# New issue times for blocks, sums, turns and attention steps in a two-layer trunk

## The chip, the cores and the metric

One core of a Trainium2 chip runs the kernel. The time is device microseconds of one execution; a kernel's time is the median of its runs. The engines are TensorE (PE, matmuls), VectorE (DVE), ScalarE (ACT), GpSimd (POOL) and SyncE (SP, which only issues transfers here). All times below are in microseconds.

## The reference

A trunk of two layers over 256 frames with 2048 features, 16 heads of 128, and an MLP width of 8192, all in float32:

```python
u = rms_norm(h, a_norm_g[l])
q, k, v, fz = jnp.split(u @ a_w_in[l], [D, 2 * D, 3 * D], axis=-1)
...                                   # q, k: rms_norm per head
logf = jax.nn.log_sigmoid(fz.astype(jnp.float32) + a_b_f[l].astype(jnp.float32))
o = forgetting_attention(q, k, v, logf)      # causal softmax, logits + cumulated logf
h = h + o.reshape(B, S, D) @ a_w_out[l]
h = h + sq_relu_mlp(h, mlp_norm_g[layer], mlp_w1[layer], mlp_w2[layer])
kv = rms_norm(h, kv_norm_g) @ kv_w           # shared keys and values
...
q = rms_norm((u @ b_w_q[l]).reshape(B, S, H, Dh), b_q_g[l])
o = chunked_relbias_attention(q, k_sh, v_sh, b_rel[l])
h = h + o.reshape(B, S, D) @ b_w_out[l]
h = h + sq_relu_mlp(h, mlp_norm_g[layer], mlp_w1[layer], mlp_w2[layer])
```

with `sq_relu_mlp(h, g, w1, w2) = square(relu(rms_norm(h, g) @ w1)) @ w2`. All weights together are read once; they are most of the traffic.

## The kernel before

**The matmuls.** A float32 product is made of three passes over rounded parts. ACT rounds a piece of weights (128 x 1024) to `hi` (L312), DVE takes the rest `lo = raw - hi` (L313), and PE runs hi times the activation's hi (L579), hi times its lo (L581) and lo times its hi (L583). One such piece with its two splits is a unit; `fetch` and `top_up` keep two or three units split ahead of PE.

**The pairs.** Two neighbouring blocks of output columns form a `Pair`. A part of its rows is multiplied in seven products in place of eight, of sums of blocks. The blocks are 11, 12, 21, 22 (loaded by SP, L911, in `bring`); the sums are T3 = 22 + 12 and T2 = T3 + 11 (DVE, L937, in `make`), T1 = 12 + 11 and T4 = T2 + 21 (in most pairs transfers of POOL that add block to block in place, L946, in `put`). The seven units of forms come in the order 11, T3, T2, T1, 21, T4, 22. T4 overwrites T2, and its transfer can be issued only when T2 has been split. `Pair.units` holds six numbers: how many plain units before the pair's first form unit the loads of 12, 22, 21 and 11, the sum T3 and the sum T1 are issued. A larger number is earlier.

**The stages.** Attention A (its projection with `plan_heads`, its softmax steps in between, its output with `plan_out`), MLP A (`plan_mlp`: pairs of the first matrix and of the second take turns), the query projection, the shared keys and values, attention B, its output, MLP B. Suffixes H and K in the tables name the two halves (H: attention A and MLP A, K: attention B and MLP B). In an MLP the first pair is "early" (W1E), the second pair of the first matrix is W1I, the rest use W1F, W1S, W2F, W2S, W2L.

**The filling steps.** Work beside the matmuls (softmax, normalization, sums of activations for the products, turns of hidden activations) is cut into steps, and `run_fill` takes steps off a queue at certain units (HM and KM: how many at each unit; ATA, ATB, LONG, SHORT, T0H, T0K: which place in the queue each step has). A turn transposes 32 x 32 blocks on DVE (L427) and moves the blocks between partitions, either by a `hop` (sixteen small transfers, L453, eight each on SP and POOL) or by a `carry` (one write to DRAM, L437, and four reads, L443).

**What sets the order.** The instructions on DVE, ACT, PE and SP are kept in the order in which the code writes them (`keep_order`), so each table fixes an order by hand: whatever stands behind a waiting instruction on its engine waits too.

Of the kernel before, what the change touches and what calls it, by code (L numbers as in the profile page):

```python
# [27 lines left out]
UN = 1024  # L28
AHEAD = 2
TABLES = {  # L30
    "ATA": ((11, 13, 15, 19, 10), (9, 12, 16, 18, 10), (8, 13, 15, 19, 9), (9, 9, 12, 12, 10)),
    "ATB": ((10, 13, 14, 18, 9), (9, 13, 15, 16, 11), (10, 12, 15, 17, 10), (7, 10, 12, 12, 9)),
# [13 lines left out]
    "LONG": ((0, 1, 2, 5, 9, 11, 11, 14, 14), (0, 0, 0, 4, 7, 9), (1, 0, 1, 3, 5, 5), (2, 0, 1, 2, 4, 5)),  # L46
    "OFH": (12, 8, 2, 7, 5, 5),
    "OFK": (11, 10, 5, 6, 8, 4),
    "ORD": {"deep1": "a4 F b4 F a5 F a6 a7", "qkv": "a2 a3 a4 F a5 F a6 F a7 b2 b3 b4", "ahead0": "F a4 F a5 a6 a7 F b4",
        "kv": "a2 F a3 a4 a5 F a6 a7 F b2 b3 b4", "deep0": "a4 F F F b4 a5 a6 a7", "ahead1": "a4 F F a5 a6 a7 F b4"},  # L50
    "OSH": (10, 11, 5, 6, 4, 2),
    "OSK": (8, 8, 6, 7, 4, 2),
    "OUTH": "F a2 a3 a4 a5 F b2 b3 F b4 G b5 G a6 a7 G b6 b7 G c2 G c3 G c4 c5 G c6 c7 d2 d3 d4",
    "OUTK": "a2 a3 F b2 a4 b3 F a5 F b4 b5 G G a6 a7 G b6 G c2 b7 G c3 G c4 c5 d2 G c6 c7 d3 d4",
    "QF": (4, 7, 1, 4, 2, 2),
    "QS": (10, 5, 4, 8, 3, 1),
    "SHORT": ((2, 0, 1, 4, 7, 7, 9, 9, 12), (2, 2, 3, 3, 7, 7, 8, 11, 13), (0, 1, 1, 4, 7, 7), (0, 0, 0, 2, 4, 4)),
# [13 lines left out]
    "XOH": (9, 12, 13, 10),  # L71
    "XOK": (9, 14, 12, 14),
    "XS": (2, 5, 4, 1),
}
EARLY = 3
LAZY = ("qkv", "kv", "out0", "out1")
# [3 lines left out]
DEEP = 2 * UN  # L80
WIDE1 = (1, 2, 3, 4, 5, 6, 7)
# [15 lines left out]
def trunk(ctx: ExitStack, tc: tile.TileContext, xT, xr, gs, hg, bf, wgate, w_in, w_oa, w1a, w1fa, w1sa, w2fa, w2sa,  # L97
          w_kv, w_qb, w_ob, w1b, w1fb, w1sb, w2fb, w2sb, rel, out):
    nc = tc.nc
    V, S, G, TE, SY = nc.vector, nc.scalar, nc.gpsimd, nc.tensor, nc.sync  # L100

    def pool(name, bufs, **kw):
        return ctx.enter_context(tc.tile_pool(name=name, bufs=bufs, **kw))
# [5 lines left out]
    qkv = pool("qkv", 2)  # L109
# [82 lines left out]
    def plan_mlp(w1, w1f, w1s, w2f, w2s, rest, when, more=None):  # L192
        pairs = []

        def add(w, wf, ws, i, wides, order, times, cols=WIDE):
            j = wides.index(i) if i in wides else i - sum(1 for k in wides if k < i)
            names = ("11", "12", "21", "22")
            if i in wides:
                m = 8 - cols // 512
                src = [[None] * (8 - m) + [ws[m * (2 * j + q) + u] for u in range(m)] for q in range(2)]  # L200
                big = {k: wf[4 * j + m] for m, k in enumerate(names)}
            else:
                src = [[w[16 * j + 8 * q + u] for u in range(8)] for q in range(2)]
                big = {k: src[int(k[1]) - 1][int(k[0]) - 1] for k in names}
            pairs.append(Pair(big, src, order, len(pairs) % 2 == 1, times, cols if i in wides else UN))

        rooms = {"12": "v0", "22": "k0", "11": "k1", "21": "v1"}
        seq = [(0, 0, 0), (0, 0, 1)]
        for c in range(NCH):
            seq += [(1, c, 0)] + [(0, c + 1, 0)] * (c + 1 < NCH) + [(1, c, 1)] + [(0, c + 1, 1)] * (c + 1 < NCH)  # L210
        for m, (second, c, q) in enumerate(seq):
            i = 2 * c + q
            if second:
                add(None, w2f, w2s, i, WIDE2, "deep%d" % q, TABLES["W2L" if i == 7 else "W2S" if q else "W2F"], DEEP)
            else:
                add(w1, w1f, w1s, i, WIDE1, "ahead%d" % q if i else "early", TABLES["W1E" + when] if not i else TABLES["W1I" + when] if i == 1 else TABLES["W1S" if q else "W1F"], DEEP)
            pairs[-1].at = second, c, q
        if more is not None:
            for q in range(2):
                add(more, None, None, q, (), "" if q else "query", TABLES["QS" if q else "QF"])  # L220
                pairs[-1].at = 1, NCH, q
        plan, rest = join(pairs, rooms, rest)
        return queue(plan + rest)

    def queue(plan):
        units.extend(Form(p, i, q == 3) if q > 1 else p.src[q][i] for p, q, i in plan)
        return plan

    def join(pairs, rooms, rest):
        plan = []  # L230
        for p in pairs:
            p.rooms = rooms
            if p.order != "early":
                rooms = {"12": rooms["11"], "22": rooms["12"], "11": rooms["21"], "21": rooms["22"]}
            mine, rest = p.plan(rest)
            plan += mine
        return plan, rest
# [33 lines left out]

    plan_h, rest, tail_h = plan_heads(w_in, "H", w_oa)
    plan_a = plan_mlp(w1a, w1fa, w1sa, w2fa, w2sa, rest, "H", w_qb)
    plan_k, rest, tail_k = plan_heads(w_kv, "K", w_ob)
    plan_b = plan_mlp(w1b, w1fb, w1sb, w2fb, w2sb, rest, "K")
    ready = deque()

# [118 lines left out]
    def room(tag, name, dtype=F32):  # L396
        return qkv.tile([P, DEEP], dtype, name=name, tag=tag, bufs=1)
# [72 lines left out]
    LONG, SHORT, SHORT2 = TABLES["LONG"], TABLES["SHORT"], TABLES["SHORT2"]  # L470
# [351 lines left out]
    early = room("bias", "early")  # L822
# [521 lines left out]
```

## Time and profile before

| what | value |
|---|---|
| median of 3 runs | 2069.12 us (2067.84 to 2071.15) |
| profiled execution | 2071.87 us, span 2070.1 us |
| granted clock of PE, mean | 0.999 |
| busy PE, DVE, ACT, POOL | 99%, 86%, 68%, 12% of the span |
| traffic | 556.20 MB, mean 269 GB/s |

A busy share is an average over stages with different limits; the waits of PE, which is busy for nearly the whole span, are read in the stage where they lie. Transfers are listed by the engine that issued them, with the time from issue to landing.

### The profile page before, as it was taken

To read this page: it belongs to the slowest core of one execution; us is meant where nothing else is said; L and a number is where in the kernel's file an instruction comes from. 1 tells how busy PE (TensorE), PEld (TensorE's weight loads), DVE (VectorE), ACT (ScalarE), POOL (GpSimd) and SP (SyncE) were. 2 spreads that over 40 slices of the span, in tenths; PEclk is the share of its full clock that TensorE was granted. 3 is DMA by queue.
4 is the path that set the end of the run, shared out by engine and by line. 5 is a ranking of instruction groups with operands and counts; after the bars stand their busy time and mean duration, and the time that the engine had idled before them with its cause. 6 is when DMAs were issued, how large, how long until landed. Compare 5 with 4: busy or idle time off the path is not lost.

```text
span 2070.1 us, 27097 instructions
## 1 busy us (share of the span) xinstructions
PE 2050.1 (99%) x9068; PEld 1689.7 (82%) x9068; DVE 1776.8 (86%) x2058; ACT 1398.8 (68%) x1799; POOL 243.9 (12%) x355
## 2 busy tenths in 40 slices
PE   9999999999999999999999999999999999999999
PEld 7888878878888888888888888888788888888887
DVE  6788788889899899899888678888998988988996
ACT  6766566667677677676778566667766675776764
POOL 1111010021101102101012011100211111111020
PEclk9999999999999999999999999999999999999999
DMA  9898888788889898897988888888888888888885
GB/s 328 258 278 273 265 262 268 281 263 256 284 270 284 252 299 274 243 286 251 285 253 262 290 260 265 256 264 284 277 284 270 267 267 286 259 284 260 288 261 148
DMA packets 174221, 556.20 MB, mean 269 GB/s; under 512 B 40688, under 2 KB 68992, under 8 KB 151040
## 3 DMA queue, kind: packets, MB, share of 16 engines
q1 hardware_dynamic: 153344, 463.94, 62.8%
q0 software_dynamic: 20448, 89.96, 21.9%
q8 instruction: 71, 1.16, 0.2%
q14 instruction: 70, 0.57, 0.1%
q10 hardware_dynamic: 288, 0.57, 0.1%
HBM read 514.50 MB, written 26.76 MB: 261 GB/s over the span
## 4 chain that ended last, share of the span: by engine, by line
PE 82%; DMA 6%; issue 5%; DVE 4%; ACT 1%; SPq 1%; POOL 0%; DVEq 0%; ACTq 0%; POOLq 0%
PE acc L579 19%; PE acc L583 19%; PE acc L581 19%; PE s L583 7%; PE s L579 7%; PE s L581 7%; DVE lo L313 2%; DMA wT<-in_w1fa 2%; ACT hi L312 1%; DMA raw<-in_w_in 1%; PE po L751 1%; DMA wT<-in_w1fb 1%; PE po L714 1%; DMA w<-in_w2fb 1%; DMA turn<-z 0%
## 5 line engine op out<-in xcount | busy, mean ns | idle before, releaser
L313 DVE TENSOR_TENSOR lo<-raw,hi 128x1024 fp32r<-128x1024 f32 (+1 forms) x414 | 500.0, 1212 | 94.6 <-ACT hi L312 86.2
L312 ACT ACTIVATE hi<-raw 128x1024 fp32r<-128x1024 f32 (+1 forms) x414 | 434.7, 1054 | 198.1 <-PE acc L581 134.2
L579 PE MATMUL acc<-hi,act 128*128 128x512 f32 x1784 | 500.1, 393 | 8.1 <-ACT hi L312 7.6
L583 PE MATMUL acc<-lo,act 128*128 128x512 f32 x1784 | 494.4, 390 | 1.3 <-DVE lo L313 1.0
L581 PE MATMUL acc<-hi,act 128*128 128x512 f32 x1784 | 493.8, 390 | 0.0
L579 PEld LDWEIGHTS acc<-hi,act 128*128 128x128 f32 x1784 | 333.4, 188 | 79.3 <-ACT hi L312 10.1
L583 PEld LDWEIGHTS acc<-lo,act 128*128 128x128 f32 x1784 | 334.1, 188 | 74.8 <-DVE lo L313 5.9
L581 PEld LDWEIGHTS acc<-hi,act 128*128 128x128 f32 x1784 | 335.3, 188 | 70.7 <-DVE act L370 0.5
L312 ACT ACTIVATE hi<-w 128x1024 fp32r<-128x1024 f32 x258 | 271.1, 1058 | 127.9 <-PE acc L581 86.5
L313 DVE TENSOR_TENSOR lo<-wT,hi 128x1024 fp32r<-128x1024 f32 x220 | 267.1, 1221 | 74.7 <-ACT hi L312 71.0
L313 DVE TENSOR_TENSOR lo<-w,hi 128x1024 fp32r<-128x1024 f32 x258 | 310.0, 1217 | 20.1 <-ACT hi L312 18.8
L312 ACT ACTIVATE hi<-wT 128x1024 fp32r<-128x1024 f32 x220 | 232.2, 1059 | 114.1 <-PE acc L581 51.8
L579 PE MATMUL s<-hi,act 128*128 128x512 f32 x530 | 146.4, 391 | 0.0
L583 PE MATMUL s<-lo,act 128*128 128x512 f32 x530 | 145.3, 389 | 0.7 <-DVE lo L313 0.7
L581 PE MATMUL s<-hi,act 128*128 128x512 f32 x530 | 144.8, 388 | 0.0
L453 POOL DMA_DIRECT2D q<-z x200 | 99.4, 512 | 251.8 <-DVE z L427 212.0
L583 PEld LDWEIGHTS s<-lo,act 128*128 128x128 f32 x530 | 99.0, 188 | 22.6 <-DVE lo L313 2.4
L581 PEld LDWEIGHTS s<-hi,act 128*128 128x128 f32 x530 | 99.4, 188 | 20.6
L579 PEld LDWEIGHTS s<-hi,act 128*128 128x128 f32 x530 | 99.1, 188 | 20.8 <-ACT hi L312 0.4
L579 PE MATMUL s<-hi,S 128*128 128x512 f32 x288 | 89.5, 392 | 0.0
L583 PE MATMUL s<-lo,S 128*128 128x512 f32 x288 | 88.9, 390 | 0.1
L581 PE MATMUL s<-hi,S 128*128 128x512 f32 x288 | 88.7, 389 | 0.0
(213 smaller groups left out, 2235.8 us busy)
## 6 DMA issues: line engine op xcount, KB each, us to landing
raw<-in_w_in SPq DMA_DIRECT2D x75, 512.0 KB, 5.8
w<-in_w2fa SPq DMA_DIRECT2D x32, 1024.0 KB, 6.4
w<-in_w2fb SPq DMA_DIRECT2D x32, 1024.0 KB, 6.2
w<-in_w1fa SPq DMA_DIRECT2D x28, 1024.0 KB, 7.2
w<-in_w1fb SPq DMA_DIRECT2D x28, 1024.0 KB, 7.0
raw<-in_w2sa SPq DMA_DIRECT2D x52, 512.0 KB, 7.7
raw<-in_w_kv SPq DMA_DIRECT2D x52, 512.0 KB, 5.2
raw<-in_w2sb SPq DMA_DIRECT2D x51, 512.0 KB, 7.0
```

Of the source, the lines that this page charges most:

```text
L312: S.activation(hi[:, c], raw[:, c], AF.Copy)
L313: V.tensor_tensor(lo[:, c], raw[:, c], hi[:, c].bitcast(F32), op=ALU.subtract)
L453: (G if i % 2 else SY).dma_start(dst[32 * j : 32 * j + 32, i * n : (i + 1) * n], z[32 * i : 32 * i + 32, j * n : (j + 1) * n])
L579: TE.matmul(ps[:, cols], xh, cut(hi, j), start=first, stop=False, **kw)
L581: TE.matmul(ps[:, cols], xl, cut(hi, j), start=False, stop=False, **kw)
L583: TE.matmul(ps[:, cols], xh, cut(lo, j), start=False, stop=last, **kw)
L714: TE.matmul(s[:, P : 3 * P], q[:, a, P:T], k[:, a], start=True, stop=True)
L751: TE.matmul(po[:, :T], v[:, 0, a * P : (a + 1) * P], pT[:, :2], start=True, stop=False)
```

## The change

Numbers in the tables of the two attention stages, the output projections and the entries of the MLPs are set anew; the tables of the MLPs' steady part stay (W1F, W1S, W2F, W2S, T). The second pair of an MLP's first matrix gets an order of its own, "second", with the same contents as the one it used. One turn of MLP B is made by a carry in place of a hop (the second number of T0K's third row, where -1 means a hop). The work is otherwise the same, instruction for instruction. Some of the lines:

```diff
-    "OFH": (12, 8, 2, 7, 5, 5),
+    "OFH": (11, 10, 1, 7, 7, 7),
...
-    "T0K": ((0, -1, 5, 5, 6, 6, 6, 7, 10), (1, -1, 4, 5, 6, 6, 6, 8, 8), (1, -1, 6, 6, 7, 7), (0, -1, 5, 5, 5, 5)),
+    "T0K": ((0, -1, 5, 5, 6, 6, 6, 7, 10), (1, -1, 5, 5, 6, 6, 7, 8, 8), (1, 3, 6, 7, 7, 7), (0, -1, 4, 4, 4, 4)),
...
-    "W1IH": (11, 7, 6, 7, 3, 2),
-    "W1IK": (10, 6, 2, 9, 4, 2),
+    "W1IH": (11, 7, 6, 9, 4, 1),
+    "W1IK": (11, 7, 3, 9, 4, 3),
...
-                add(w1, w1f, w1s, i, WIDE1, "ahead%d" % q if i else "early", TABLES["W1E" + when] if not i else TABLES["W1I" + when] if i == 1 else TABLES["W1S" if q else "W1F"], DEEP)
+                add(w1, w1f, w1s, i, WIDE1, ("second" if i == 1 else "ahead%d" % q) if i else "early", TABLES["W1E" + when] if not i else TABLES["W1I" + when] if i == 1 else TABLES["W1S" if q else "W1F"], DEEP)
```

The changed file is one line longer, so a line there has a number one higher than the same line before.

Three places in the order. The first is SP just ahead of the forms of MLP A's second pair. `w11`, `w22` and `w21` are that pair's blocks, `raw` and `zraw` plain units, `turn` and `q` the last turn of attention A's output. Before:

```order
L437 DMA turn_3643<-z_3639 128x1024
L291 DMA raw_3659<-in_w1a 128x1024
L291 DMA raw_3695<-in_w1a 128x1024
L443 DMA q_3640<-turn_3643 32x4x256 x4
L911 DMA w22_3713<-in_w1fa 128x2048
L911 DMA w11_3715<-in_w1fa 128x2048
L291 DMA raw_3727<-in_w1a 128x1024
```

And after:

```order
L438 DMA turn_3643<-z_3639 128x1024
L912 DMA w11_3645<-in_w1fa 128x2048
L292 DMA raw_3661<-in_w1a 128x1024
L292 DMA raw_3693<-in_w1a 128x1024
L444 DMA q_3640<-turn_3643 32x4x256 x4
L912 DMA w22_3715<-in_w1fa 128x2048
L292 DMA raw_3727<-in_w1a 128x1024
```

The load of block 11 moved ahead of two plain units and the four reads of the turn.

The second place is DVE in attention A, about 105 us into the span. `row` and `pbuf` belong to the softmax of earlier heads, `t` to that of the next ones, `acc` is a sum in an accumulator of the running pair (L976). Before:

```order
L313 TENSOR_TENSOR lo_996<-raw_866,hi_995 128x1024
L734 RECIPROCAL row_968<-row_968 128x2
L736 TENSOR_SCALAR pbuf_123<-pbuf_123,row_968 128x128
L736 TENSOR_SCALAR pbuf_123<-pbuf_123,row_968 128x256
L427 STREAM_TRANSPOSE pbuf_123<-pbuf_123 128x3x4x32
L723 SCALAR_TENSOR_TENSOR t_1017<-po_990,cq_753,nb_803 128x128
L725 TENSOR_REDUCE row_1018<-t_1017 128x1
L723 SCALAR_TENSOR_TENSOR t_1017<-po_990,cq_753,nb_803 128x256
L725 TENSOR_REDUCE row_1018<-t_1017 128x1
L976 SCALAR_TENSOR_TENSOR acc_1034<-acc_921,p7_980 128x512
L313 TENSOR_TENSOR lo_1038<-R_358,hi_1037 128x1024
L313 TENSOR_TENSOR lo_1046<-raw_904,hi_1045 128x1024
```

And after:

```order
L314 TENSOR_TENSOR lo_989<-raw_877,hi_988 128x1024
L977 SCALAR_TENSOR_TENSOR acc_1020<-acc_927,p7_980 128x512
L314 TENSOR_TENSOR lo_1024<-R_358,hi_1023 128x1024
L735 RECIPROCAL row_968<-row_968 128x2
L737 TENSOR_SCALAR pbuf_123<-pbuf_123,row_968 128x128
L737 TENSOR_SCALAR pbuf_123<-pbuf_123,row_968 128x256
L428 STREAM_TRANSPOSE pbuf_123<-pbuf_123 128x3x4x32
L724 SCALAR_TENSOR_TENSOR t_1031<-po_1008,cq_753,nb_794 128x128
L726 TENSOR_REDUCE row_1032<-t_1031 128x1
L724 SCALAR_TENSOR_TENSOR t_1031<-po_1008,cq_753,nb_794 128x256
L726 TENSOR_REDUCE row_1032<-t_1031 128x1
L314 TENSOR_TENSOR lo_1042<-raw_903,hi_1041 128x1024
```

The accumulator's sum and one split moved ahead of the eight softmax instructions.

The third place is DVE some 150 us later, at the first output pair of attention A. `wT3` is that pair's sum T3, `y` a sum of head outputs. Before:

```order
L427 STREAM_TRANSPOSE pbuf_123<-pbuf_123 128x3x4x32
L313 TENSOR_TENSOR lo_2490<-raw_2355,hi_2489 128x1024
L937 TENSOR_TENSOR wT3_2507<-R_238,R_358 128x1024
L313 TENSOR_TENSOR lo_2517<-raw_2402,hi_2516 128x1024
L1083 TENSOR_TENSOR y_2525<-act_1211 128x256 x4
```

And after, where the sum now stands:

```order
L314 TENSOR_TENSOR lo_2399<-raw_2292,hi_2398 128x1024
L938 TENSOR_TENSOR wT3_2417<-R_238,R_358 128x1024
L314 TENSOR_TENSOR lo_2427<-wT3_2112,hi_2426 128x1024
L735 RECIPROCAL row_2341<-row_2341 128x2
L737 TENSOR_SCALAR pbuf_123<-pbuf_123,row_2341 128x128
```

T3 moved ahead of two groups of softmax instructions and four splits.

More of the change, by code (lines that the diff above doesn't have):

```diff
@@ L30 @@
 TABLES = {
-    "ATA": ((11, 13, 15, 19, 10), (9, 12, 16, 18, 10), (8, 13, 15, 19, 9), (9, 9, 12, 12, 10)),
-    "ATB": ((10, 13, 14, 18, 9), (9, 13, 15, 16, 11), (10, 12, 15, 17, 10), (7, 10, 12, 12, 9)),
[1 row of a table removed]
+    "ATA": ((11, 13, 15, 19, 9), (9, 12, 16, 18, 11), (8, 13, 15, 19, 9), (9, 9, 12, 12, 10)),
+    "ATB": ((10, 13, 14, 18, 9), (9, 13, 15, 17, 11), (9, 12, 15, 17, 10), (7, 10, 12, 12, 9)),
[1 row of a table added]
     "GS": (1,),
[11 rows of a table removed]
-    "LONG": ((0, 1, 2, 5, 9, 11, 11, 14, 14), (0, 0, 0, 4, 7, 9), (1, 0, 1, 3, 5, 5), (2, 0, 1, 2, 4, 5)),
-    "OFH": (12, 8, 2, 7, 5, 5),
[L48 to L57, printed above, removed]
[1 row of a table removed]
[11 rows of a table added]
+    "LONG": ((0, 1, 2, 5, 9, 10, 11, 14, 14), (0, 0, 0, 4, 7, 9), (1, 0, 1, 2, 5, 5), (1, 0, 1, 4, 5, 5)),
+    "OFH": (11, 10, 1, 7, 7, 7),
+    "OFK": (10, 9, 4, 9, 8, 4),
[3 rows of a table added]
+    "OSH": (7, 9, 7, 5, 5, 1),
+    "OSK": (9, 7, 4, 7, 5, 1),
+    "OUTH": "F a2 a3 b2 a4 a5 b3 b4 F G F G b5 a6 a7 G b6 b7 G c2 G c3 G d2 c4 c5 G c6 c7 d3 d4",
+    "OUTK": "a2 a3 F b2 a4 F b3 a5 F b4 b5 G G a6 a7 G b6 G c2 b7 d2 G c3 G c4 c5 c6 G c7 d3 d4",
+    "QF": (4, 4, 2, 3, 2, 1),
+    "QS": (10, 4, 4, 8, 3, 1),
+    "SHORT": ((4, 0, 0, 3, 6, 8, 8, 9, 12), (2, 2, 3, 3, 7, 7, 8, 10, 13), (2, 0, 0, 2, 6, 7), (0, 0, 0, 2, 4, 5)),
[1 row of a table added]
     "T": ((1, -1, 5, 14, 14, 14, 15, 20, 20), (0, 2, 8, 10, 10, 14, 18, 20, 22), (0, -1, 5, 6, 7, 7), (0, -1, 4, 5, 5, 5)),
[4 rows of a table removed]
[4 rows of a table added]
     "W1F": (7, 5, 1, 5, 4, 3),
[2 rows of a table removed]
[2 rows of a table added]
     "W1S": (8, 6, 4, 5, 4, 1),
     "W2F": (6, 5, 1, 5, 4, 3),
[1 row of a table removed]
[1 row of a table added]
     "W2S": (7, 7, 4, 5, 3, 1),
-    "XOH": (9, 12, 13, 10),
+    "XOH": (9, 12, 13, 11),
     "XOK": (9, 14, 12, 14),
-    "XS": (2, 5, 4, 1),
+    "XS": (0, 5, 6, 2),
 }
```

35 rows, old and new, of the table TABLES are left out of this document.

## Prediction

> **What bounds the kernel now.** I read the head of the page, then the waits of PE (the engine of the matmuls), then the timeline around each wait.
>
> ```profile
> span 2070.1 us, 27097 instructions
> PE 2050.1 (99%) x9068; PEld 1689.7 (82%) x9068; DVE 1776.8 (86%) x2058; ACT 1398.8 (68%) x1799; POOL 243.9 (12%) x355
> PE acc L579 <- ACT hi L312: 7.6, 6, 3.4
> PE acc L583 <- DVE lo L313: 2.6, 3, 1.2
> PE acc L579 <- DVE acc L976: 1.4, 1, 1.4
> PE acc L579 <- ACT pbuf L731: 1.1, 1, 1.1
> PE pt L138 <- DVE mhalf L140: 1.1, 1, 1.1
> PE s L583 <- DVE lo L313: 0.7, 2, 0.4
> ```
>
> PE is busy for 99% of the span and the change keeps every matmul, so PE's own work is a floor. What a new order can win is the waits. The columns of the last six lines are total us, times, longest: together 14.5 us. The change can only move these, or make new ones. Where they lie (start, duration, instruction, in brackets the idle time before it and its releaser):
>
> ```profile
> 107.05 0.47 PE L579 MATMUL acc<-hi,S 128*128 128x512 f32 x1 [1.13 <-ACT pbuf L731]
> 279.39 0.49 PE L583 MATMUL acc<-lo,act 128*128 128x512 f32 x1 [0.99 <-DVE lo L313]
> 442.21 0.92 PE L579 MATMUL acc<-hi,act 128*128 128x512 f32 x2 [3.37 <-ACT hi L312]
> 1465.34 0.73 PE L579 MATMUL acc<-hi,act 128*128 128x512 f32 x2 [1.18 <-ACT hi L312]
> 1481.81 0.50 PE L583 MATMUL s<-lo,act 128*128 128x512 f32 x1 [0.37 <-DVE lo L313]
> 468.68 0.50 PE L583 MATMUL acc<-lo,Sh 128*128 128x512 f32 x1 [0.40 <-DVE lo L313]
> ```
>
> The longest costs more than its wait. In the windows below (PE busy with count, PEld, DVE, ACT, POOL, granted clock, DMA share, GB/s) the clock falls to 0.83 right behind it.
>
> ```profile
> 400.00:410.00 10.00, 10.00 (x46) 8.28 (x45) 3.62 (x4) 5.16 (x9) 0.00 (x0) 1.00 1.00 407
> 420.00:430.00 10.00, 9.95 (x44) 7.73 (x43) 9.97 (x10) 6.96 (x9) 2.47 (x5) 1.00 0.79 222
> 430.00:440.00 10.00, 8.84 (x40) 6.98 (x38) 8.40 (x12) 5.84 (x6) 3.46 (x7) 1.00 1.01 269
> 440.00:450.00 10.00, 7.79 (x27) 6.23 (x28) 7.16 (x7) 8.09 (x9) 0.50 (x1) 0.83 0.75 276
> 1460.00:1470.00 10.00, 8.75 (x37) 6.35 (x36) 8.63 (x12) 6.95 (x9) 0.97 (x2) 1.00 0.87 267
> ```
>
> 46 matmuls fill 10 us, 0.217 us each. From 442.21 to 450 there are 7.8 us, room for 36, and 27 ran: 9 x 0.217 = 2.0 us lost to the clock. The wait of 442.21 is therefore worth 3.37 + 2.0 = 5.4 us, and the ceiling for the whole change is 14.5 + 2.0 = 16.5 us.
>
> **Part 1, the second pair of MLP A (W1IH, T0H).** The chain of waits and the timeline name a transfer, the POOL accumulate that makes form T4:
>
> ```profile
> 426.83 14.17 DMA wT<-in_w1fa
> 595.83 11.11 DMA wT<-in_w1fa
> 923.01 11.48 DMA wT<-in_w1fa
> wT<-in_w1fa POOLq DMA_DIRECT2D x7, 1024.0 KB, 9.2
> 426.83 0.92 POOL L946 DMA_DIRECT2D wT<-in_w1fa  x1 [2.69 <-DVE lo L313]
> 431.61 10.69 SPq L453 DMA_DIRECT2D q<-z  x8
> 397.51 0.85 SPq L911 DMA_DIRECT2D w<-in_w1fa  x2
> 390.61 0.33 SPq L437 DMA_DIRECT2D turn<-z  x1
> ```
>
> It left at 426.83 and landed at 441.00, after 14.17 us, where its likes took 11.11 and 11.48 when they were late and 9.2 in the median (last column). Around it the DMA engines were full (share 1.01 from 430 to 440) while 420 to 430 still had a fifth free; the sixteen turn pieces issued from 431.61 share them. The change brings the load of the 1 MB block "11", one of the two issued at 397.51, forward past two raw loads and the reads of a turn, right behind the row of 390.61: some 6.5 us sooner. It leaves the full stretch of 400 to 410, where DVE worked 3.62 us of 10, waiting for what comes behind. Also the T3 sums move ahead of a weight split, into that idle time. I take DVE's chain and the turn behind it to run 2 us earlier, which leaves more of the traffic before 430. T4 itself can hardly leave sooner: POOL waited 2.69 us for the split of the form that T4 overwrites, and that split goes at PE's pace. So I take 11.5 us, the row of 923.01, for its flight: it lands at 438.3, and the wait falls from 3.37 to 3.37 - 2.7 = 0.7. The window of 1460 to 1470, with its wait of 1.18, kept the clock at 1.00, so the 2.0 us go too. Gain 2.7 + 2.0 = 4.7; I take 4.4, since what lands sooner here has to be split sooner too. Bounds 0 (it still takes 14.17) and 5.4 (9.2 lands at 436.0, and 3.37 before 441.0 is 437.6).
>
> The Trainium skill, "DMA: Bandwidth & Descriptors", section "Queues, rings and completion order", says that each DMA engine takes turns between the queues it has work for, a packet at a time. By that T4's share depends on whether SP's queue has work at all, not on how much, and a load that left earlier helps only if SP's queue then runs empty; the sum would lose the 4.4. The row of 14.17 against 9.2 speaks for a share that varies, but not for which cause. This is the first rival.
>
> **Part 2, attention A's steps (ATA, ATB, HM).** The profile names ACT's L731 as the releaser at 107.05, but on DVE the sum of L976, which frees the bank that the matmul writes, ended at 106.91, just ahead of it:
>
> ```profile
> 103.54 0.16 DVE L734 RECIPROCAL row<-row 128x2 f32<-128x2 f32 x1
> 106.22 0.69 DVE L976 SCALAR_TENSOR_TENSOR acc<-acc,p 128x512 f32<-128x512 f32 x1
> 107.94 1.22 DVE L313 TENSOR_TENSOR lo<-raw,hi 128x1024 fp32r<-128x1024 f32 x1
> ```
>
> Between 103.54 and 106.22 stand eight softmax instructions, 2.7 us; they hold up L976. The change puts L976 and one split ahead of the eight, so the wait of 1.13 goes. What is late next is the split behind the eight (the row of 107.94, ended at 109.16): it ends about as before, but PE is there 1.1 us sooner; I charge 0.3. Net 0.8; bounds -0.3 (if ACT's L731 was the releaser after all) and 1.1.
>
> **Part 3, first output pair of A (OFH).** The T3 sum leaves a stretch in which DVE has no pause for one in which it had some:
>
> ```profile
> 264.86 1.22 DVE L937 TENSOR_TENSOR wT<-R 128x1024 f32<-128x1024 f32 x1
> 254.55 1.23 DVE L313 TENSOR_TENSOR lo<-wT,hi 128x1024 fp32r<-128x1024 f32 x1 [0.66 <-ACT hi L312]
> 261.33 1.23 DVE L313 TENSOR_TENSOR lo<-R,hi 128x1024 fp32r<-128x1024 f32 x1 [1.40 <-ACT hi L312]
> ```
>
> It moves to just ahead of the row at 254.55. Of its 1.22 us, 0.66 fall into that pause, the rest into the one of 1.40 before 261.33; up to there it delays two splits by up to 1.2 us. DVE then reaches 279 up to 1.22 us sooner, and PE's wait there is 0.99. I take 1.0; bounds 0 and 1.2.
>
> **Part 4, MLP B's second pair (W1IK) and its sums (T0K).** T4 of this pair gated PE at 1465.34. The order of DVE and SP from 1441 to 1465 stays; only T1's accumulate and the load of "21" before it come earlier, so some of the traffic is gone sooner: 0.4 of 1.18, bounds 0 and 1.2. Behind it four sums move from ahead of the split that PE waited for to behind two splits:
>
> ```profile
> 1477.88 0.41 DVE L382 TENSOR_TENSOR sum<-q 128x256 f32<-128x256 f32 x1
> ```
>
> Four of 0.41 are 1.6 us, more than the 0.37 that PE waited at 1481.81: gain 0.4.
>
> **Part 5, the rest.** One hop (sixteen small transfers) of MLP B becomes a write to DRAM and four reads, all on SP:
>
> ```profile
> 1480.68 4.99 SPq L453 DMA_DIRECT2D q<-z  x8
> 1495.81 1.04 ACT L1009 ACTIVATE q<-q 128x1024 f32<-128x1024 f32 x1
> turn<-z SPq DMA_DIRECT2D x35, 512.0 KB, 5.2
> q<-turn SPq DMA_DIRECT2D x68, 128.0 KB, 5.6
> ```
>
> A write at 1480.7 and reads behind it land 5.2 + 5.6 later plus SP's rows between, at 1492 to 1494, before ACT wants them at 1495.81: nothing, and without that cover the difference, up to 2 us on ACT, which is not PE's bound there. At 468.68, in the pair behind Part 1, the split that PE waits for keeps its place, with ACT and DVE steps of the activation now ahead of it: cost 0.2. About thirty weight loads leave 1 to 9 us later in the issue order; those I followed keep their cover, because the split they feed is 2 to 6 us ahead of PE. One that doesn't costs about what the smaller waits above cost, 0.4 to 1.2; I charge one, 0.8 (bounds 0 and 4).
>
> **The sum.** 4.4 + 0.8 + 1.0 + 0.4 + 0.4 - 0.2 - 0.8 = 6.0 us. The profiled execution took 2071.87 us (span 2070.1 and 1.8 around it), 2.75 above the median of 2069.12; it becomes 2065.9, and the median 2063.1.
>
> **The rivals.**
>
> *T4 does not land sooner.* The moved megabyte was long down when T4 left, and SP's queue still has the turn and the blocks of the second matrix to send. For it: 0.79 share in 420 to 430 says the engines had no backlog from 400 then. Against it: the chain ahead of the turn starts sooner. The gain is 6.0 - 4.4 = 1.6, time 2067.5, within 0.2%. Chance 0.18.
>
> *T4 takes longer, and it ends slower.* If the turn's sixteen pieces are done sooner, SP goes on sooner to what now follows:
>
> ```profile
> 442.41 1.00 SPq L911 DMA_DIRECT2D w<-in_w2fa  x2
> ```
>
> These two 1 MB loads left just after T4 had landed. Issued 3 us sooner they run beside T4's last part. With 2 MB at the 407 GB/s of the fullest window its flight grows by 5.2 us, PE waits 8.6 and the low clock lasts twice as long: +5.2 + 2.0, less the other gains' 1.6, is 5.6 us slower, 2074.7. Against it: SP issues them only when their buffers are free. It decides from a landing at 442.6 on (441.0 plus those 1.6). Chance 0.10, with 0.08 more for a late load elsewhere that does the same to PE.
>
> **How the numbers follow.** Forecast (T4 lands sooner and no new wait beyond the one charged): 2063.1, chance 0.64. All upper bounds together are 5.4 + 1.1 + 1.2 + 1.2 + 0.4 = 9.3, plus the run's own spread of 1.3 to 2.0: low end 2057.5. The high end takes in the first rival with its spread and the lighter part of the second: 2072. About a fifth is left outside. 0.2% is 4.1 us, what a measurement of this kernel can tell from no change; the line is at 2065.0 and 2073.3. The forecast's own range, 2058 to 2067, lies partly above 2065.0; I give 0.54 of its 0.64 to faster and 0.10 to same, which with the first rival makes 0.28. The second rival and its kin are the 0.18 of slower.
>
> **What would show it.** In the profile after: the accumulate of "wT" issued near 425 lands in under 12 us; PE's wait behind it is under 1 us; the clock is 1.00 in every window of the second pair. No wait on L731 near 107, none on L313 near 279 and near 1480. I am wrong if the total of PE's waits does not fall below 9 us, if a new wait above 1.5 us stands on ACT's L312 behind a load or an accumulate, or if the clock drops anywhere else.

## The result and the profile after

The changed kernel takes 2063.25 us (median of 7 runs, 2061.24 to 2066.70) against 2070.95 (7 runs, 2064.83 to 2071.26) on the same chip. The ratio is 0.9971, 95% interval 0.9961 to 0.9982: 6.0 us faster, between 3.7 and 8.1 (the two medians lie 7.7 apart; the ratio takes in all the runs). The forecast was 2063.1. The profile after is of the fastest of its seven executions (2061.24), the one before of an execution slower than any of its seven (2071.87), so the two spans lie 10.7 us apart and show more than the gain.

The head of the page and the waits of PE in the profile after (line numbers are one higher):

```profile
span 2059.4 us, 27087 instructions
PE acc L580 <- ACT hi L313: 3.9, 6, 1.4
PE acc L584 <- DVE lo L314: 2.3, 3, 1.0
PE pt L139 <- DVE mhalf L141: 1.1, 1, 1.1
PE s L584 <- DVE lo L314: 0.3, 1, 0.3
PE acc L580 <- ACT act L756: 0.2, 1, 0.2
```

The listed waits fell from 15.3 us (the 14.5 shown before and three small ones) to 7.8, and the longest from 3.4 to 1.4. The waits on L976 and L731 are gone. The one on L976 stood at 1745 us, in the steady part of MLP B, whose tables stay; E1, E6, E8 and E10 below, which leave MLP B as before, don't have it either, so its end is not the change's gain. The place behind the T4 accumulate of MLP A's second pair, in the timeline, the list of transfers (last column: us to landing) and the windows:

```profile
421.24 0.93 POOL L947 DMA_DIRECT2D wT<-in_w1fa  x1 [4.17 <-DVE lo L314]
wT<-in_w1fa POOLq DMA_DIRECT2D x1, 1024.0 KB, 12.4
434.88 0.50 PE L580 MATMUL acc<-hi,act 128*128 128x512 f32 x1 [1.37 <-ACT hi L313]
430.00:440.00 10.00, 8.57 (x37) 6.48 (x36) 9.53 (x12) 7.31 (x9) 0.50 (x2) 1.00 0.86 268
440.00:450.00 10.00, 10.00 (x46) 8.29 (x45) 9.83 (x11) 6.77 (x7) 0.92 (x1) 1.00 0.87 288
```

T4 flew 12.4 us and not 14.17, PE waited 1.37 and not 3.37, and the clock stayed at 1.00: 46 matmuls in the window that held 27. Read from these two profiles alone, Part 1 of the prediction looks right. The experiments say otherwise.

### The profile page after: what moved, and what is told of

It is laid out like the page before. It is cut to its first block, busy times and chain, and to the rows that moved or that the text cites. A ratio compares the mean times of both kernels' runs of the same rounds, so it can differ in the third digit from the quotient of the medians.

```text
span 2059.4 us, 27087 instructions
## 1 busy us (share of the span) xinstructions
PE 2047.2 (99%) x9068; PEld 1689.5 (82%) x9068; DVE 1777.7 (86%) x2058; ACT 1399.3 (68%) x1799; POOL 238.8 (12%) x347
## 3 DMA queue, kind: packets, MB, share of 16 engines
q8 instruction: 71, 1.16, 0.2%
## 4 chain that ended last, share of the span: by engine, by line
PE 91%; DVE 3%; issue 2%; DMA 2%; ACT 1%; SPq 0%; ACTq 0%; POOL 0%; DVEq 0%; POOLq 0%
PE acc L584 21%; PE acc L580 21%; PE acc L582 21%; PE s L580 9%; PE s L582 9%; PE s L584 9%; DVE lo L314 1%; DMA wT<-in_w1fb 1%; PE po L715 1%; PE po L752 1%; ACT hi L313 1%; DMA q<-turn 0%; DMA raw<-in_w2sb 0%; PE po L714 0%; PE po L753 0%
```

## The experiments

Each was run beside the kernel before on one chip; ratios are to that. Before's own median was between 2068.57 and 2070.95 in these comparisons, so the ratio with its interval counts and not the difference of two medians from different ones.

**E1: W1IH alone.**

```diff
-    "W1IH": (11, 7, 6, 7, 3, 2),
+    "W1IH": (11, 7, 6, 9, 4, 1),
```

> The kernel before with only W1IH from the change. Theory (the T4 accumulate of MLP A's second pair lands sooner because the load of block 11, T3's sums and what follows them come earlier): the wait near 440 falls from 3.37 to about 1.5 us and the clock stays at 1.00 behind it, 4 us faster than before (2065 to 2067), all other waits as before. Rival (the other tables of attention A bring it, by an earlier SP and DVE ahead of the pair): the wait stays above 3 us and the clock falls, within 1 us of before.

Ratio 1.0014 (1.0004 to 1.0025): 2.9 us slower. The wait behind T4 fell to 2.18, but another stood ahead of it. Timeline of E1 (PE, ACT) and its list of transfers for the turn's reads; then the same two rows of before:

```profile
409.84 0.50 PE L579 MATMUL acc<-hi,act 128*128 128x512 f32 x1 [1.75 <-ACT hi L312]
406.05 0.51 ACT L404 ACTIVATE y<-q,gsb 128x256 f32<-128x256 f32 x1 [3.99 <-DMA q<-turn]
q<-turn SPq DMA_DIRECT2D x4, 128.0 KB, 9.7
```

```profile
400.61 1.71 ACT L404 ACTIVATE y<-q,gsb 128x256 f32<-128x256 f32 x4 [0.29 <-DMA q<-turn]
q<-turn SPq DMA_DIRECT2D x4, 128.0 KB, 4.1
```

The megabyte of block 11 now flies ahead of the turn's reads. They take 9.7 us in place of 4.1, ACT waits for them 3.99 us with the next weight splits behind it, and PE runs dry. In this profile the new wait of 1.75 and the 1.19 less behind T4 make 0.6 of the 2.9 us; where the rest lies was not traced. Neither theory had this; it is the first step of the prediction that failed.

**E2: the tables of attention A and its output alone** (ATA, HF, HM, HS, XS, OFH, OSH, OUTH, XOH and the order "qkv" from the change).

> The kernel before with only the tables of attention A and its output (ATA, HF, HM, HS, XS, OFH, OSH, OUTH, XOH and the order qkv). Theory: the waits near 107 (1.13) and 279 (0.99) go, the wait of 3.37 near 440 stays with its low clock; 2 to 3 us faster than before. Rival (the attention tables bring the pair's transfers forward): the wait near 440 falls below 2 us as well and the run is 6 us faster.

Ratio 0.9984 (0.9974 to 0.9994): 3.3 us faster. The waits near 107 and 279 are gone, and the wait behind T4 was 1.88 with the clock at 1.00, though W1IH was as before.

**E3: the tables of the second half alone** (ATB, KM, KF, KS, KX, LONG, SHORT, SHORT2, OFK, OSK, OUTK, QF, QS, T0K, W1EK, W1IK, W2L and the order "kv").

> The kernel before with only the tables of the second half (query, keys and values, attention B, its output, entry of MLP B). Theory: the waits of the first half stay, 0.3 to 1 us faster (the wait near 1481 goes, those near 1030 and 1465 stay or shrink). Rival (late loads in attention B cost what the rest gains): 1 us slower or more, with new waits between 1000 and 1480.

Ratio 0.9987 (0.9975 to 0.9999): 2.7 us faster, more than expected, though the interval reaches almost to nothing. This group holds SHORT, which times the normalizations ahead of MLP A as well, so that this kernel differs from before from about 340 us on. The wait behind T4 was 2.28 here and not 3.37, with the clock down as before:

```profile
440.50 0.79 PE L579 MATMUL acc<-hi,act 128*128 128x512 f32 x1 [2.28 <-ACT hi L312]
440.00:450.00 10.00, 9.50 (x35) 7.75 (x36) 8.88 (x8) 7.82 (x10) 0.07 (x1) 0.83 0.77 285
```

Whether SHORT has a part in the 2.28 can't be said: E10, E11 and E12, with before's tables at this place, had 2.71 to 2.89.

**E4: all of the change but W1IH.**

> The changed kernel with W1IH as before. Theory: the wait near 435 is back at about 3.4 us and the clock falls behind it; 3 to 4 us slower than the changed kernel (about 2067). Rival: the wait stays near 1.4 us and the time within 1 us of the changed kernel.

Ratio 0.9974 (0.9963 to 0.9984), against 0.9971 with W1IH. The wait was back, with its low clock, and the time was the same:

```profile
437.03 0.80 PE L579 MATMUL acc<-hi,act 128*128 128x512 f32 x1 [2.89 <-ACT hi L312]
430.00:440.00 10.00, 7.11 (x26) 5.49 (x25) 7.38 (x10) 5.74 (x7) 1.14 (x3) 0.83 0.80 205
```

In the change W1IH is worth nothing that these runs can tell: the two ratios differ by 0.6 us, and each is known to about 2 us.

**E5: the whole first half alone** (E2's tables with W1IH, T0H and W1EH).

> The kernel before with the tables of attention A, its output, and the entry of MLP A (W1IH, T0H, W1EH). Theory (the attention tables give about 3 us; W1IH's earlier load of block 11 delays the last turn's reads, which costs only where the turn has no room): no wait near 405 as with W1IH alone, the wait behind T4 near 437 at 1.5 us with a full clock; 3 to 4 us faster than before, as with the attention tables alone or up to 1 us better. Rival (W1IH is worth 4 us once the turn has room): 6 us or more faster.

Ratio 0.9980 (0.9966 to 0.9995), 4.1 us, not to be told from E2. The theory that the attention tables make room for the turn fell. The wait of E1 stands here too, and the clock falls behind it:

```profile
406.40 0.50 PE L579 MATMUL acc<-hi,act 128*128 128x512 f32 x1 [2.00 <-ACT hi L312]
402.61 1.71 ACT L404 ACTIVATE y<-q,gsb 128x256 f32<-128x256 f32 x4 [4.01 <-DMA q<-turn]
400.00:410.00 10.00, 8.00 (x31) 6.22 (x30) 4.56 (x5) 6.50 (x9) 0.00 (x0) 0.89 1.02 402
q<-turn SPq DMA_DIRECT2D x4, 128.0 KB, 9.2
```

Up to MLP A's last pair this kernel and the changed one differ in SHORT alone. In the profile after, the reads took 7.8 us (7.1 in E4, without the new W1IH), and ACT's rows at this place are others:

```profile
398.56 0.91 ACT L405 ACTIVATE y<-q,gsb 128x256 f32<-128x256 f32 x2 [2.94 <-DMA q<-turn]
399.38 1.04 ACT L313 ACTIVATE hi<-raw 128x1024 fp32r<-128x1024 f32 x1
400.32 0.89 ACT L405 ACTIVATE y<-q,gsb 128x256 f32<-128x256 f32 x2
q<-turn SPq DMA_DIRECT2D x4, 128.0 KB, 7.8
```

SHORT takes the four normalizations in two pairs with a weight split between them, 4 us sooner, so the split that PE needs next no longer stands behind all four. The wait is in the two kernels with the new W1IH and the old SHORT (E1 1.75, E5 2.00), and in neither with both new (the change, E7). What makes W1IH harmless at the turn is therefore SHORT, by elimination: the two were not run together without the rest.

**E6: before, with one load later.** The 1 MB of block 12 for the first pair of the second matrix left SP 0.7 us ahead of T4. One unit later it stands behind the turn's pieces. The part of the line that changes:

```diff
-TABLES["W2L" if i == 7 else "W2S" if q else "W2F"]
+((5, 5, 1, 5, 4, 3) if i == 0 and when == "H" else TABLES["W2L" if i == 7 else "W2S" if q else "W2F"])
```

> The kernel before with one number changed: the first pair of MLP A's second matrix loads its block 12 one unit later, so SP issues it behind the turn's pieces and not 0.7 us ahead of the T4 accumulate. Theory (T4's flight of 14.17 us is stretched by the megabyte in front of it): T4 flies 9 to 11 us, the wait near 442 is under 1 us with a full clock, and the run is 2 to 4 us faster, less what the later load costs behind it. Rival (T4's flight is stretched by the turn's sixteen pieces or is what an accumulate takes): T4 flies 12 us or more and the time is within 1 us of before.

Ratio 0.9990 (0.9978 to 1.0001), 2 us, not clear of none. Timeline and transfer: T4 flew 11.4 us, PE waited 0.54, the clock stayed at 1.00.

```profile
wT<-in_w1fa POOLq DMA_DIRECT2D x1, 1024.0 KB, 11.4
437.95 0.50 PE L579 MATMUL acc<-hi,act 128*128 128x512 f32 x1 [0.54 <-ACT hi L312]
```

In before, then, the megabyte in front of T4 stretched its flight by 2.3 to 2.8 us (it is 13.7 to 14.2 in before, E10, E11 and E12).

**E7: the changed kernel with E6's edit.**

> The changed kernel with the same one number changed (block 12 of the second matrix's first pair one unit later). Theory: T4's flight falls from 12.42 to 9 to 10 us, the wait near 435 goes, 1 to 1.5 us faster than the changed kernel (2062). Rival: no shorter flight, or a new wait near 450 where the pair needs block 12: at or above 2063.5.

2063.62 us, ratio 0.9974 (0.9963 to 0.9986): no gain over the change, though T4's wait fell to 0.67. T4 flew 11.7 us, 0.7 less than in the change. Another wait, of 1.16, stood where MLP B begins, on the normalization of its activations (L408); E4 (1.01) and E6 (1.28) have the like and the change has not, and what brings it stays open:

```profile
1425.91 1.20 PE L580 MATMUL acc<-hi,act 128*128 128x512 f32 x4 [1.16 <-ACT act L408]
```

**E8: before, with the turn beside T4 made by DRAM** (T0H, second row: 3 for -1).

> The kernel before with the second turn of MLP A's first chunk made by a write to DRAM and four reads (T0H, second row, second number 3) in place of sixteen small pieces beside T4. If the pieces stretch T4, it flies 11 us or less in place of 14.17 and the wait near 442 falls below 1 us. If T4 holds up what is issued behind it and not the other way round, it flies 13 to 14 us as before, the wait stays at 2 to 3.5 us, and the turn's reads land only after T4 has landed.

Ratio 1.0015 (1.0001 to 1.0029), 3 us slower. SP was free to issue the two loads that the second rival was about while T4 flew. Timeline, then the transfers issued between 425.7 and 435.3:

```profile
431.01 4.16 SPq L911 DMA_DIRECT2D w<-in_w2fa  x2
wT<-in_w1fa POOLq DMA_DIRECT2D x1, 1024.0 KB, 12.9
w<-in_w2fa SPq DMA_DIRECT2D x2, 1024.0 KB, 11.0
raw<-in_w1sa SPq DMA_DIRECT2D x2, 512.0 KB, 11.9
```

T4 flew 12.9 us, no longer than before. What left behind it took 11 to 12 us in the median and landed after it. So two megabytes issued while it flew did not stretch T4; they waited. Without the sixteen pieces, with a write of 512 KB in their place, the flight lies within the 12.7 to 14.2 us of the runs that have them and the old W1IH (table below), so no effect of theirs shows either. Part of the 3 us stands behind the pair, where two splits now come late for PE (before had no wait there):

```profile
456.45 0.73 PE L583 MATMUL s<-lo,S 128*128 128x512 f32 x2 [0.62 <-DVE lo L313]
459.99 1.20 PE L583 MATMUL s<-lo,act 128*128 128x512 f32 x4 [0.97 <-DVE lo L313]
```

**E9: all of the change but W1IH, with E6's edit.**

> The changed kernel with W1IH as before and with block 12 of MLP A's first second-matrix pair loaded one unit later. Theory (W1IH takes from the wait behind T4 about what it adds at the turn near 405, and the later load takes from T4's flight without that price): no wait near 405 above 0.5 us, T4 flies 11 to 12 us, its wait is under 1 us, 1 to 2 us faster than the changed kernel (2061 to 2062). Rival (the medians move with transfers elsewhere): within 1 us of the changed kernel.

2062.34 us, ratio 0.9966 (0.9954 to 0.9977), the best of all, faster than before and 1 us under the change by ratio, which the intervals don't tell apart. T4 flew 11.0 us and PE waited 0.19 for it, but 2.3 us later 1.09 for the second split, which DVE issued behind four sums:

```profile
wT<-in_w1fa POOLq DMA_DIRECT2D x1, 1024.0 KB, 11.0
433.87 0.73 PE L579 MATMUL acc<-hi,act 128*128 128x512 f32 x2 [0.19 <-ACT hi L312]
436.17 0.50 PE L583 MATMUL acc<-lo,act 128*128 128x512 f32 x1 [1.09 <-DVE lo L313]
434.56 0.42 DVE L385 TENSOR_TENSOR sum<-q,sum 128x256 f32<-128x256 f32 x1
434.89 2.35 DVE L313 TENSOR_TENSOR lo<-wT,hi 128x1024 fp32r<-128x1024 f32 x2
```

A transfer that lands sooner meets the next thing in the written order. E7 and E9 differ in W1IH alone, and the kernel without it is the faster by 1.7 us, within the intervals: here too W1IH shows no gain.

**E10: ATA and HM alone.**

> The kernel before with only ATA and HM, which put the accumulator's sum ahead of the eight softmax instructions near 105 us. Theory: the wait of 1.13 behind L731 near 107 goes and nothing comes in its place, 1 to 1.7 us faster. Rival (the split behind the eight is late in its turn): a wait of 0.3 to 1 us near 109.

Ratio 0.9995 (0.9986 to 1.0005). In its timeline PE has no wait between 105 and 112, so the wait of 1.13 went and none took its place; in time it can't be told from nothing. The wait itself is beyond doubt: it is there in all seven profiles with the old ATA and HM (1.13 to 1.56) and in none of the seven with the new.

**E11: OFH alone** (the fifth row of the diff in front).

> The kernel before with only OFH: the sum T3 of attention A's first output pair 9 us earlier. Theory: the waits between 277 and 288 fall from about 2.2 us in all to about 1, 1 us faster. Rival: DVE is as late at 279 as before and the waits stay near 2 us.

Ratio 0.9993 (0.9984 to 1.0002), 1.4 us, not clear of none. Between 276 and 290 one wait of PE is left, that of 0.35; the 0.99 near 279 is gone. One such profile would not settle it, for the waits at this place vary, but all of them do: between 270 and 295 PE waits 0.7 to 3.0 us in the seven with the old OFH and 0 to 0.6 in the seven with the new.

```profile
282.86 1.21 PE L583 MATMUL s<-lo,act 128*128 128x512 f32 x4 [0.35 <-DVE lo L313]
```

**E12: T0K, W1IK, W1EK and W2L alone.**

> The kernel before with only T0K, W1IK, W1EK and W2L. Theory: the wait of the split near 1481 goes (0.5 us) and the one behind T4 near 1465 shrinks by up to 0.5, in all 0.5 to 1 us faster. Rival (the gain of the second half came from the query projection): both waits as before, no faster.

Ratio 1.0005 (0.9993 to 1.0017): no gain. Between 1460 and 1495 only the wait behind T4 is left, as long as before; the one of the split is gone, as in all six profiles with these tables, while the other eight have it (0.37 to 0.42). The wait behind this T4 runs from 0.96 to 2.27 in those eight and up to 1.74 in the six, too wide to read Part 4's 0.4 from it.

```profile
1469.22 0.73 PE L579 MATMUL acc<-hi,act 128*128 128x512 f32 x2 [1.17 <-ACT hi L312]
```

The T4 of MLP A's second pair in all the runs, ordered by what the code has at that place:

| run | W1IH | block 12 ahead of T4 by, us | flight, us | PE's wait, us | lowest clock in the windows 430 to 450 |
|---|---|---|---|---|---|
| before | old | 0.7 | 14.2 | 3.37 | 0.83 |
| E3 | old | 0.5 | 13.3 | 2.28 | 0.83 |
| E10 | old | 1.4 | 13.8 | 2.71 | 0.85 |
| E11 | old | 0.7 | 13.7 | 2.89 | 0.83 |
| E12 | old | 0.8 | 13.7 | 2.88 | 0.87 |
| E4 | old | 0.6 | 13.7 | 2.89 | 0.83 |
| E2 | old | 0.9 | 12.7 | 1.88 | 1.00 |
| E8 (turn by DRAM) | old | 0.7 | 12.9 | 2.09 | 0.83 |
| E1 | new | 1.5 | 13.1 | 2.18 | 0.83 |
| E5 | new | 2.7 | 12.0 | 0.96 | 1.00 |
| change | new | 2.5 | 12.4 | 1.37 | 1.00 |
| E6 | old | behind it | 11.4 | 0.54 | 1.00 |
| E7 | new | behind it | 11.7 | 0.67 | 1.00 |
| E9 | old | behind it | 11.0 | 0.19 | 1.00 |

With the load ahead, the new W1IH takes about 1.1 us off the wait (mean of 2.62 in eight profiles without it, 1.50 in three with it), and the clock fell in seven of the eight and in one of the three. The two groups overlap: E2's 1.88 lies below E1's 2.18. The table also suggests how: with the new W1IH the load of block 12 left SP 1.5 to 2.7 us ahead of T4, without it 0.5 to 1.4, and the two flights with the longest lead are shorter than all others with that load ahead. That this is what W1IH does at T4 was not tested. With the old SHORT, W1IH gives the 1.1 us back at the turn near 406, by waits of 1.75 in E1 and 2.00 in E5.

## Why the prediction was right, and where it was not

The time, its sign and the range were right. That the sum hit the time is luck, for two of its errors cancel: Part 1's 4.4 us does not show in the time, and the rest brought 3.8 more than its 1.6.

**Part 1 (4.4 us) failed.** The step was to let the load of block 11 pass "two raw loads and the reads of a turn" and to price only what it leaves, not what it is put ahead of. The reads it passed went from 4.1 us to 9.7 in E1 and 9.2 in E5. Alone W1IH costs 2.9 us (E1); in the change SHORT, which the prediction did not weigh at this place, takes the wait away (by elimination), and even so W1IH is worth nothing measurable (E4 against the change, E9 against E7). The mechanism was half right: T4 does land sooner and the clock stays up. But the flight of 11.5 us that the sum took needs the megabyte of block 12 behind T4 (11.4 in E6, 11.7 in E7, 11.0 in E9), which the change does not do; and what is saved at T4 does not show in the kernel's time (E4).

**The rest was undersized.** Without Part 1 the sum left 1.6 us. E4, the change without W1IH, gained 5.4 (3.3 to 7.7). It keeps T0H and W1EH of MLP A's entry, which were run only together with W1IH (E5, not to be told from E2); the gains of E2 and E3 add to 6.0 without them. Attention A's tables brought 3.3 where Parts 2 and 3 had 1.8. Their two waits went as forecast: E10 and E11, each unclear in time by itself, add to 2.4 (1.0 and 1.4, each with about 2 us of uncertainty); the rest of the 3.3 was not taken apart. The second half brought 2.7 (0.2 to 5.2) where Part 4 less the rest gave about nothing. It does not come from MLP B's entry (E12), whose split no longer waits as Part 4 said while its T4 waits as before. Whether SHORT brings it at MLP A's entry, or the query, key, value and attention B tables later, was not taken apart and stays open.

**Part 5 was not contradicted.** The turn made by DRAM cost nothing that E12 could show, within about 2.5 us. The 0.8 charged for a late load was not found: the profile after has two new waits at MLP B's entry (0.57 near 1450 and 0.81 near 1456), but E4, E7 and E9 don't have them, and neither was followed to a load. The low end of the range is off by 0.3: 2069.1 - 9.3 - 2.0 is 2057.8.

**The rivals.** T4 landing sooner without an effect on the time is close to what W1IH did, by another mechanism than the rival's. The second rival's price is refuted by E8: two megabytes issued while T4 flew left its flight at 12.9 us. But a slower kernel was near: E1 is one, by a load that blocks a turn.

**The signs.** PE's waits fell below 9 us, no wait above 1.5 us appeared and the clock held, as forecast, and near 107 and 1480 no wait is left (near 279 one of 0.35 is); T4's flight (12.4, not under 12) and its wait (1.37, not under 1) missed the bounds set for them.

The Trainium skill's rule ("DMA: Bandwidth & Descriptors", "Queues, rings and completion order") has each engine take turns between queues. In the runs T4 did not slow when SP's queue had more to send (E8), which agrees with it so far. Taking turns alone does not tell why in before a 512 KB load that left 0.6 us behind T4, with half of its bytes, took 14.3 us and landed 0.8 after it; in E6, without the megabyte ahead of it, the like took 9.8 and landed 1.0 before T4.

The load of before, in the timeline and the list of transfers:

```profile
427.43 0.33 SPq L291 DMA_DIRECT2D raw<-in_w1sa  x1
raw<-in_w1sa SPq DMA_DIRECT2D x1, 512.0 KB, 14.3
```

## What to carry to other kernels

When a transfer is moved forward, price every transfer it is put ahead of, down to the engine that waits for them in order; here one megabyte doubled the flight of four small reads, and alone it cost more than it won. Undo the part that carries most of a forecast even when the total agrees: two profiles showed the wait shrink, and only the kernel without that part showed that its gain could not be told from nothing. And follow a table to every place where it is read: one that was counted to the second half cleared, by elimination, a stall that another had made in the first.

## What the hardware showed unexpectedly

The granted clock fell behind waits of PE of 2.0 us and more near T4 and the turn (E5's 2.00, E8's 2.09, E1's 2.18; also behind E11's 2.19 near 8 us, to 0.88), and not behind those of 1.75 (E1) and 1.88 (E2): far shorter waits than the one of 3.37 from which the prediction took it. That length alone doesn't decide it is seen in MLP B's entry of E5, where a wait of 2.27 near 1464 left the clock up. Whatever SP and POOL issued while T4 flew landed behind it or, at the earliest, 1.0 us ahead of it (E6). The megabyte of block 12 lengthened T4's flight by 2.8 us where it was issued 0.7 us ahead of it (before against E6), by 2.7 at 0.6 (E4 against E9) and by 0.7 at 2.5 (the change against E7). The same wait with the same tables around it differs by up to 0.7 us between profiles (T4's in before, E10, E11 and E12: 2.71 to 3.37), and by more near 280 us (0.7 to 3.0 in all in before, E1, E6, E8 and E12).
